# Two heads' memory queries join the key chunk, and the turns of the probabilities open the next memory step

## The chip, the cores and the metric

The kernel runs on one core of a Trainium2 chip. The metric is the device time of one execution in microseconds (us), lower is better. The engines named here are TensorE (PE in the profile, PEld for its weight loads), VectorE (DVE), ScalarE (ACT), GpSimd (POOL), and SyncE (SP), which issues DMAs. "Product" means one matmul of the program.

## The reference

Two layers of a decoder trunk on 512 tokens of width 1024, in f32. One projection `h @ w_in` feeds four branches. The change touches how two of them start, sparse attention (its keys, values and index queries) and cross-attention to a memory of 256 tokens:

```python
h = rmsnorm(x, norm_mix)
(a_x, a_b, a_c, d_q, d_k, d_v, i_q, i_k, i_w,
 g_q, g_f, g_i, g_g, m_q, gate_logits) = split_cols(h @ w_in)
y_a = a_b * causal_conv3(a_c * a_x, conv_w)
...
mq = rmsnorm(m_q.reshape(b, s, MEM_HEADS, MEM_HEAD_DIM), mem_q_norm)
ml = jnp.einsum('bshd,bmhd->bhsm', mq, mk).astype(jnp.float32) * (MEM_HEAD_DIM ** -0.5)
mp = jax.nn.softmax(ml, axis=-1).astype(mv.dtype)
y_m = jnp.einsum('bhsm,bmhd->bshd', mp, mv)
```

There are four memory heads of 128. The branches are lifted to the model's width, gated and summed, then follow an output projection, the residual and a gated FFN.

## The kernel before

Activations `h` lie feature-major: 8 blocks of 128 features by 512 tokens. Each f32 value is held as a high and a low half, and each product of two such values is three matmuls (`mm3`, L316, L317, L319: high by high, high by low, low by high). Weights come in chunks (`wchunk`): SP loads a part of 128 x 1024 raw values (four buffers), ScalarE rounds it to the high half, VectorE subtracts to get the low half (three buffers each).

A chunk is used in one of two ways. *Feature-major* (`features`): 128 columns of the weight are stationary and the 512 tokens of `h` move; the result has features on partitions. *Token-major* (`tokens`, `tokens_wide`): 128 tokens of `h` are stationary and up to 512 weight columns move; the result has tokens on partitions. `tokens` does one block of tokens after the other, `tokens_wide` takes all four blocks part by part of the weights, with an accumulator bank each. In the profile a row `mm<-h,w` is feature-major and `mm<-w,h` token-major. Eight PSUM banks serve as accumulators: three `mm`, three `tr`, two `at`.

The stretch in question is the beginning of the mixer of each layer. Three generators, written as a sequence of steps, are advanced by a string, `EARLY` (L46), letter by letter in `script`: `b` the projections of sparse attention, `c` the convolution branch, `m` the memory branch, `n` the row of norms by token (`late_norm`), `s` the selection. The string sets the order of emission; a scheduler then orders each engine's instructions by their priority and by when it takes them to be ready.

- `b`, first step: the key chunk, 256 columns (keys, values, first index queries) as four blocks by `tokens`. `key_out` evicts each block into a tile `wide` by ScalarE, scaled by the token norm `r_t`; `key_heads` normalises, rotates and transposes it (two transposes a block at L929). Later steps are the index chunk (456 columns) and the query chunk (512), both by `tokens_wide`.
- `c`, six steps of 256 columns by `features`; the evictions multiply by the norm row `r_b` (L709).
- `m`, ten steps: for each pair of heads one step with the queries (256 columns by `features`, their high and low halves, squares, four matmuls a head at L762 for the mean squares, the norm `rs`), then four steps, each half the tokens of one head: scores, maximum, exponentials, their sum and scaling (L796), four transposes of the probabilities (L798, the *turns*), products with the memory values, eviction.

In layer 1 the token norm comes first: `norm_token` (matmuls at L378) gives `r_t`, which is stored to DRAM by the ScalarE queue (L367) and loaded back as a row on all partitions by SP (L369).

`tc.add_manual_dep(..., order, ...)` sets an order of two instructions of an engine or a queue.

## Time and profile before

| | us |
|---|---|
| three runs | 1957.14, 1957.16, 1957.38 |
| median | 1957.16 |
| profiled execution | 1957.13 |
| its span, first to last instruction | 1955.4 |

The page of the profile gives busy times of the engines, the span in slices, the queues, the chain of work that ended last, and the costliest groups. Times within the trace count from the start of the span. The duration of a matmul's row is longer than its share of PE, since matmuls are pipelined: 394 ns in the largest group, while its rows start about 0.23 us apart. The DMA engines moved 386.79 MB, 198 GB/s over the span.

### The profile page before, as it was taken

The page shows a single profiled execution, that of the slowest core. Times are in us where ns is not written, and L with a number is a line of the kernel's source. Part 1 is how long each engine was busy: PE and PEld are TensorE (multiplying, and loading weights), DVE is VectorE, ACT ScalarE, POOL GpSimd, SP SyncE. Part 2 cuts the span into 40 slices and gives each one's busy share as a digit, 9 for nine tenths or more (in the row PEclk, how much of TensorE's full clock was granted, in tenths as well). Part 3 has the DMA queues.
Part 4 walks back from the last instruction along what each step waited for, and adds up shares of the span by engine and source line. Part 5 has one row for each costly group of instructions (what it writes and reads, how often), then busy time and mean ns, then how long its engine had stood idle before and what let it go on. Part 6 is the DMA issues. An engine that isn't in the chain of part 4 may idle for free.

```text
span 1955.4 us, 26140 instructions
## 1 busy us (share of the span) xinstructions
PE 1949.9 (100%) x9443; PEld 1618.5 (83%) x9443; DVE 1453.9 (74%) x2552; ACT 1166.1 (60%) x1944; POOL 232.0 (12%) x281
## 2 busy tenths in 40 slices
PE   9999999999999999999999999999999999999999
PEld 7888888878888888888888888888888888888887
DVE  7765899667776776786876688985778667867677
ACT  8654564866764556655644547477667556556464
POOL 1011111111111111110001111111111110111000
PEclk9999999999999999999999999999999999999999
DMA  9576767767777889886687776766667779898864
GB/s 365 189 185 165 178 152 171 159 143 156 178 204 193 240 229 247 248 255 191 200 215 164 180 170 157 170 163 151 153 171 177 207 199 260 240 271 249 238 187 140
DMA packets 221043, 386.79 MB, mean 198 GB/s; under 512 B 13809, under 2 KB 114417, under 8 KB 220657
## 3 DMA queue, kind: packets, MB, share of 16 engines
q1 hardware_dynamic: 162000, 247.69, 40.1%
q0 software_dynamic: 51568, 130.96, 33.2%
q10 hardware_dynamic: 7344, 6.47, 1.0%
q8 instruction: 74, 1.21, 0.3%
q14 instruction: 57, 0.46, 0.1%
HBM read 372.48 MB, written 138.42 MB: 261 GB/s over the span
## 4 chain that ended last, share of the span: by engine, by line
PE 98%; DVE 1%; DMA 0%; ACT 0%; SPq 0%; issue 0%
PE mm L316 24%; PE mm L319 24%; PE mm L317 24%; PE at L316 4%; PE at L317 4%; PE at L319 4%; PE tr L316 2%; PE tr L319 2%; PE tr L317 2%; PE tr L872 1%; PE at L832 1%; PE at L831 1%; PE tr L1592 1%; PE tr L861 1%; PE tr L929 0%; DMA w_raw<-in_mem_w_kv_dram 0%
## 5 line engine op out<-in xcount | busy, mean ns | idle before, releaser
L101 ACT ACTIVATE w_hi<-w_raw 128x1024 fp32r<-128x1024 f32 (+1 forms) x435 | 457.6, 1054 | 367.8 <-PE mm L317 129.1
L316 PE MATMUL mm<-h_hi,w_hi 128*128 128x512 f32 x960 | 378.1, 394 | 0.0
L317 PE MATMUL mm<-h_lo,w_hi 128*128 128x512 f32 x960 | 376.6, 392 | 0.0
L319 PE MATMUL mm<-h_hi,w_lo 128*128 128x512 f32 x960 | 372.8, 394 | 0.0
L1286 DVE TENSOR_TENSOR w_lo<-w_raw,w_hi 128x1024 fp32r<-128x1024 f32 x211 | 256.5, 1219 | 129.9 <-ACT w_hi L101 129.2
L245 DVE TENSOR_TENSOR w_lo<-w_raw,w_hi 128x1024 fp32r<-128x1024 f32 (+1 forms) x224 | 272.7, 1218 | 95.7 <-ACT w_hi L101 95.1
L1301 POOL DMA_DIRECT2D up_sums<-in_ffn_w_up_dram x120 | 121.4, 1012 | 832.0 <-DMA up_sums<-in_ffn_w_up_dram 561.9
L316 PEld LDWEIGHTS mm<-h_hi,w_hi 128*128 128x128 f32 x960 | 180.5, 188 | 36.5 <-DVE zq L1074 0.8
L319 PEld LDWEIGHTS mm<-h_hi,w_lo 128*128 128x128 f32 x960 | 180.2, 188 | 36.1 <-DVE w_lo L245 0.5
L317 PEld LDWEIGHTS mm<-h_lo,w_hi 128*128 128x128 f32 x960 | 180.5, 188 | 35.3
L319 PE MATMUL mm<-w_hi,h_lo 128*128 128x512 f32 (+2 forms) x408 | 151.7, 373 | 0.0
L317 PE MATMUL mm<-w_lo,h_hi 128*128 128x512 f32 (+2 forms) x408 | 151.7, 372 | 0.0
L316 PE MATMUL mm<-w_hi,h_hi 128*128 128x512 f32 (+2 forms) x408 | 145.6, 372 | 0.0
L1301 POOL DMA_DIRECT2D w_sums<-in_ffn_w_down_dram x66 | 62.3, 944 | 327.1 <-DMA w_sums<-in_ffn_w_down_dram 193.8
L316 PEld LDWEIGHTS mm<-w_hi,h_hi 128*128 128x128 f32 x408 | 76.8, 188 | 12.2 <-ACT w_hi L101 0.2
L317 PEld LDWEIGHTS mm<-w_lo,h_hi 128*128 128x128 f32 x408 | 76.9, 188 | 12.1
L319 PEld LDWEIGHTS mm<-w_hi,h_lo 128*128 128x128 f32 x408 | 76.9, 188 | 11.7
L319 PE MATMUL mm<-y_hi,w_lo 128*128 128x512 f32 x192 | 75.7, 394 | 0.0
L317 PE MATMUL mm<-y_lo,w_hi 128*128 128x512 f32 x192 | 75.3, 392 | 0.0
L316 PE MATMUL mm<-y_hi,w_hi 128*128 128x512 f32 x192 | 75.1, 393 | 0.0
L101 ACT ACTIVATE prob<-prob,small 128x128 f32<-128x128 f32 (+3 forms) x128 | 68.9, 553 | 10.3 <-DVE small L847 6.2
L317 PE MATMUL mm<-w_lo,a_hi 128*128 128x512 f32 (+1 forms) x163 | 64.0, 393 | 0.0
(462 smaller groups left out, 4193.2 us busy)
## 6 DMA issues: line engine op xcount, KB each, us to landing
w_raw<-in_w_in_dram SPq DMA_DIRECT2D x140, 512.0 KB, 4.7
up_sums<-in_ffn_w_up_dram POOLq DMA_DIRECT2D x120, 512.0 KB, 6.9
w_raw<-up_sums SPq DMA_DIRECT2D x80, 512.0 KB, 5.3
w_raw<-in_ffn_w_up_dram SPq DMA_DIRECT2D x60, 512.0 KB, 5.0
w_sums<-in_ffn_w_down_dram POOLq DMA_DIRECT2D x54, 512.0 KB, 6.6
up_sums<-up_sums POOLq DMA_DIRECT2D x40, 512.0 KB, 5.2
w_raw<-in_w_lift_dram SPq DMA_DIRECT2D x32, 512.0 KB, 4.7
w_raw<-in_ffn_w_down_dram SPq DMA_DIRECT2D x24, 512.0 KB, 5.1
```

What stands on the lines that cost most here:

```text
L101: i = act.activation(dst, src, func, **kw)
L245: i2 = dve.tensor_sub(lo, raw, f(hi))
L316: made += [pe.matmul(ps, ah, bh, start=first, stop=False, skip_group_check=more), pe.matmul(ps, ah, bl, start=False, stop=False, skip_grou ...
L317: pe.matmul(ps, ah, bl, start=False, stop=False, skip_group_check=more)]
L319: made += [pe.matmul(ps, al, bh, start=False, stop=last, skip_group_check=more)]
L831: return [pe.matmul(ps, q[:, hh, s], k[0][:, :n], start=True, stop=False), pe.matmul(ps, q[:, hh, s], k[1][:, :n], start=False, stop=True)]
L832: pe.matmul(ps, q[:, hh, s], k[1][:, :n], start=False, stop=True)]
L861: turn = pe.transpose(pp[:, (2 * e + i) * P:(2 * e + i + 1) * P], probs[2 * i + e][:, b * P:(b + 1) * P], ident)
L872: i = pe.matmul(pv[e * HD:(e + 1) * HD, c], vt[:, b, :], pt[:, b, e * 2 * P:(e + 1) * 2 * P], start=b == 0, stop=b == t)
L1286: two = A(hi, raw, AF.Copy), dve.tensor_sub(lo, raw, f(hi))
L1301: i = nc.gpsimd.dma_start(dst, src, **kw)
L1592: turns.extend(pe.transpose(ps[:, t * P:(t + 1) * P], us[t][:, j * P:(j + 1) * P], ident) for t in range(NT))
```

## The change

One weight chunk of 512 columns takes the 256 columns of keys and the 256 columns of the first two memory heads' queries, from two places of `w_in`, and is used token-major by `tokens_wide`, with the three `mm` banks and one `at` bank. `key_out` evicts the queries unscaled as well, squares them, and VectorE sums the squares to `mean_sq`. The first memory step transposes the queries, two heads by four blocks, back to feature-major, and has no chunk, no squares and no matmuls for the mean squares of its own. The second pair of heads is left as it was. In layer 1 the matmuls of the token norm are ordered behind the second of the chunk's four parts.

A memory step now yields behind the scaling; the turns, the products with the values and the evictions open the next step. The turns of a step are ordered behind the 24th matmul of the convolution chunk before it. `b` comes first in `EARLY` and has one step more. In layer 0 the move of the norm row (`row_moves[2]`) is ordered behind the second exponential instead of the fourth. The spacer of the constants shrinks by the 64 bytes that `mean_sq` takes.

```diff
-EARLY = ["mnmbmcmcbmmmsccbmscmbscmbsbbss", "mnmbmcmcbmmmsccbmscmbscmbsbbss"]
+EARLY = ["bnmbcmcmcmbmmmscbmscmbscmbsbbss", "bnmbcmcmcmbmmmscbmscmbscmbsbbss"]
...
-    consts.tile([P, 320], U8, name="spacer")
+    consts.tile([P, 256], U8, name="spacer")
...
-                if len(src.shape) == 2:
+                if isinstance(src, tuple):
+                    for g in range(2):
+                        nc.sync.dma_start(raw.rearrange("p k (g c) -> p k g c", g=2)[:, :, g, :],
+                                          src[g][k * P:e * P].rearrange("(k p) n -> p k n", p=P))
+                elif len(src.shape) == 2:
...
-    def tokens_wide(ws, a, kt, pss, first=0, in_turn=False):
+    def tokens_wide(ws, a, kt, pss, first=0, in_turn=False, marks=None):
...
                 behind_part = made[-1]
+                if marks is not None:
+                    marks.append(behind_part)
...
         def script(steps, gens):
+            filler = None
             for c in steps:
+                recent.clear()
+                turns.clear()
                 next(gens[c], None)
+                if c == "m" and filler is not None:
+                    for i in turns:
+                        tc.add_manual_dep(i.ins, filler.ins.name, order, reason="products first")
+                elif c == "c" and len(recent) >= 40:
+                    filler = recent[23]
...
-                w = wchunk(w_in[l][:, C_MQ + q * 256:C_MQ + (q + 1) * 256], KD, 256)
+                if q:
+                    w = wchunk(w_in[l][:, C_MQ + q * 256:C_MQ + (q + 1) * 256], KD, 256)
...
-                pqs = features(w, h, (0, 1))
+                if q:
+                    pqs = features(w, h, (0, 1))
+                else:
+                    pqs = [tr_ps() for _ in range(2)]
+                    for j, pq in enumerate(pqs):
+                        for t, u in enumerate(first_queries):
+                            pe.transpose(pq[:, t * P:(t + 1) * P], u[:, (2 + j) * P:(3 + j) * P], ident)
...
-                    sq = scratch512(S)
                     with tc.high_priority(offset=AHEAD):
-                        i = A(qh, pq, AF.Copy, scale=col(74 + l))
-                        if l == 0 and q == 0 and j == 0:
-                            after_two.append(i)
-                        A(sq, pq, AF.Square)
+                        A(qh, pq, AF.Copy, scale=col(74 + l))
+                        if q:
+                            sq = scratch512(S)
+                            A(sq, pq, AF.Square)
                         dve.scalar_tensor_tensor(ql, pq, col(74 + l), f(qh), op0=OP.mult, op1=OP.subtract)
-                    pm = tr_ps()
-                    for t in range(NT):
-                        pe.matmul(pm[:, t:t + 1], sq[:, t * P:(t + 1) * P], ones_h[:, 0:1], start=True, stop=True)
+                    if q:
+                        pm = tr_ps()
+                        for t in range(NT):
+                            pe.matmul(pm[:, t:t + 1], sq[:, t * P:(t + 1) * P], ones_h[:, 0:1], start=True, stop=True)
                     ms, rs = small(NT), small(NT, "mrs", 3)
-                    dve.tensor_mul(ms, pm[:, :NT], r2)
+                    dve.tensor_mul(ms, pm[:, :NT] if q else mean_sq[:, j, :], r2)
...
-                            if len(exps) == 4:
+                            if len(exps) == 2:
                                 tc.add_manual_dep(row_moves[2].ins, e.ins.name, order, reason="probabilities first")
...
                         dve.reciprocal(sm, sm)
+                        for i, p in enumerate(prs):
+                            scaled.append(dve.tensor_scalar(p, p, sm[:, i:i + 1], None, op0=OP.mult))
+                        yield
                         pp = tr_ps()
                         for i, p in enumerate(prs):
-                            scaled.append(dve.tensor_scalar(p, p, sm[:, i:i + 1], None, op0=OP.mult))
                             for b in range(2):
-                                pe.transpose(pp[:, (2 * b + i) * P:(2 * b + i + 1) * P], p[:, b * P:(b + 1) * P], ident)
+                                turns.append(pe.transpose(pp[:, (2 * b + i) * P:(2 * b + i + 1) * P], p[:, b * P:(b + 1) * P], ident))
...
-                        yield
...
                 def key_out(ps, t):
-                    u = wide()[:, :4 * HD]
+                    u = wide()
                     with tc.high_priority(offset=AHEAD):
                         A(vt[:, t, :], ps[:, HD:2 * HD], AF.Copy, scale=r_t[:, t:t + 1])
                         A(u[:, HD:2 * HD], ps[:, 0:HD], AF.Copy, scale=r_t[:, t:t + 1])
-                        A(u[:, 2 * HD:], ps[:, 2 * HD:4 * HD], AF.Copy, scale=r_t[:, t:t + 1])
+                        A(u[:, 2 * HD:4 * HD], ps[:, 2 * HD:4 * HD], AF.Copy, scale=r_t[:, t:t + 1])
+                        A(u[:, 4 * HD:], ps[:, 4 * HD:], AF.Copy)
+                    sq = scratch512(S)[:, :2 * P]
+                    A(sq, u[:, 4 * HD:], AF.Square, scale=P ** -0.5)
+                    dve.tensor_reduce(mean_sq[:, :, t], sq.rearrange("p (a b) -> p a b", b=P), axis=AX.X, op=OP.add)
                     return u
...
                 def projections():
-                    w = wchunk(w_in[l][:, C_DK:C_DK + 256], KD, 256)
-                    for t in range(NT):
-                        ps = mm_ps()[:, :256]
-                        tokens(w, h, t, ps)
-                        key_heads(key_out(ps, t), t)
+                    w = wchunk((w_in[l][:, C_DK:C_DK + 256], w_in[l][:, C_MQ:C_MQ + 256]), KD, 512)
+                    pss = [mm_ps() for _ in range(MM_BUFS)] + [at_ps()]
+                    marks = []
+                    tokens_wide([w], h, KD, pss, in_turn=True, marks=marks)
+                    for i in token_norm if l else ():
+                        tc.add_manual_dep(i.ins, marks[1].ins.name, order, reason="products first")
+                    first_queries.extend(key_out(ps, t) for t, ps in enumerate(pss))
+                    yield
+                    for t, u in enumerate(first_queries):
+                        key_heads(u, t)
                     yield
```

`mm3` collects its matmuls in `recent`, and `norm_token` its own in `token_norm`.

More of the change, by code (lines that the diff above doesn't have):

```diff
@@ L307, in tokens_wide @@
                 behind_part = made[-1]
+                if marks is not None:
+                    marks.append(behind_part)
             k0 += w.kt
+    recent, turns = [], []
     def mm3(ps, a, b, first, last, more=False, part=None):
@@ L319, in mm3 @@
             made += [pe.matmul(ps, al, bh, start=False, stop=last, skip_group_check=more)]
+        recent.extend(made)
         return made
@@ L373, in hybrid_trunk @@
     after_split = []
+    token_norm = []
     def norm_token(ssq):
         ps = tr_ps()
+        token_norm.clear()
         for t in range(NT):
-            pe.matmul(ps[:, t:t + 1], ssq[:, t * P:(t + 1) * P], ones_d, start=True, stop=True)
+            token_norm.append(pe.matmul(ps[:, t:t + 1], ssq[:, t * P:(t + 1) * P], ones_d, start=True, stop=True))
         r = small(NT, name="rstd_t", bufs=2)
@@ L698, in weave @@
                 pass
-        scaled = []
+        scaled, first_queries, mean_sq = [], [], None
         def conv_branch(y):
@@ L950, in key_out @@
                         A(u[:, HD:2 * HD], ps[:, 0:HD], AF.Copy, scale=r_t[:, t:t + 1])
-                        A(u[:, 2 * HD:], ps[:, 2 * HD:4 * HD], AF.Copy, scale=r_t[:, t:t + 1])
+                        A(u[:, 2 * HD:4 * HD], ps[:, 2 * HD:4 * HD], AF.Copy, scale=r_t[:, t:t + 1])
[3 more added lines that the diff above has]
+                    dve.tensor_reduce(mean_sq[:, :, t], sq.rearrange("p (a b) -> p a b", b=P), axis=AX.X, op=OP.add)
                     return u
                 def key_heads(u, t):
+                    u = u[:, :4 * HD]
                     w = by_head(u)
@@ L1029, in projections @@
                         yield
+                mean_sq = small(2 * NT, "mean_sq", 2).rearrange("p (j t) -> p j t", t=NT)
                 y_m, y_a = new_y(), new_y()
```

## The prediction

> **What bounds the kernel now.** I read the page first: the span, the busy times, the chain that ended last.
>
> ```profile
> span 1955.4 us, 26140 instructions
> ...
> PE 1949.9 (100%) x9443; PEld 1618.5 (83%) x9443; DVE 1453.9 (74%) x2552; ACT 1166.1 (60%) x1944; POOL 232.0 (12%) x281
> ...
> PE 98%; DVE 1%; DMA 0%; ACT 0%; SPq 0%; issue 0%
> ```
>
> TensorE is busy from one end to the other and is 98% of the chain. A busy PE can still hide lost time, since a matmul's row overlaps the next one's. So the second view is the table of waits, for PE alone (who waited for whom: us in total, times, the longest), and the third the stretches that the change touches: 54 to 82 us in layer 0 and 1003 to 1032 us in layer 1, from the first memory queries to the end of the key chunk (columns: length; PE, weight loads, VectorE, ScalarE, GpSimd busy with counts; clock; DMA share; GB/s).
>
> ```profile
> PE tr L149 <- DVE one L131: 1.2, 1, 1.2
> PE mm L317 <- DVE w_lo L245: 0.4, 1, 0.4
> PE mm L524 <- ACT w_hi L101: 0.4, 1, 0.4
> ```
>
> ```profile
> 54.00:82.00 28.00, 27.98 (x191) 25.63 (x190) 19.58 (x69) 18.55 (x49) 3.79 (x8) 1.00 0.69 224
> 1003.00:1032.00 29.00, 29.00 (x193) 26.58 (x192) 18.72 (x55) 17.41 (x49) 2.25 (x3) 1.00 0.90 187
> ```
>
> The table lists three waits, 2.0 us in the whole run, none at a turn of the probabilities (L798). PE is busy 27.98 of 28.00 us and 29.00 of 29.00 us at the full granted clock (1.00). So nothing can be won here by hiding a wait. What the change is worth is how much PE time its own instructions need, and whether a wait appears where none is. Starts in the timeline, not durations, give what a matmul costs a busy PE.
>
> **The change part by part.** First the rows of layer 0 (start, duration, engine, line, operation; x counts merged rows), and the group rows of PE for 70.68 to 76.80 us and for 185.8 to 189.3 us, which give counts.
>
> ```profile
> 54.26 0.48 PE L316 MATMUL mm<-h_hi,w_hi 128*128 128x512 f32 x1
> ...
> 55.04 0.39 PE L317 MATMUL mm<-h_lo,w_hi 128*128 128x512 f32 x1
> 55.45 0.50 PE L319 MATMUL mm<-h_hi,w_lo 128*128 128x512 f32 x1
> 55.78 0.39 PE L316 MATMUL mm<-h_hi,w_hi 128*128 128x512 f32 x1
> ...
> 65.56 0.28 PE L316 MATMUL mm<-w_hi,h_hi 128*128 128x256 f32 x1
> ...
> 67.35 0.95 PE L762 MATMUL tr<-ones_h,sq 128*128 128x1 f32 x8
> 68.16 0.36 PE L317 MATMUL mm<-w_lo,h_hi 128*128 128x256 f32 x1
> 68.36 0.28 PE L319 MATMUL mm<-w_hi,h_lo 128*128 128x256 f32 x1
> ...
> 70.69 0.28 PE L317 MATMUL mm<-w_lo,h_hi 128*128 128x256 f32 x1
> ...
> 76.81 0.60 PE L798 MATMUL tr<-ident,mprob 128*128 128x128 f32 x4
> 77.16 0.36 PE L317 MATMUL mm<-w_lo,h_hi 128*128 128x256 f32 x1
> 77.36 0.28 PE L319 MATMUL mm<-w_hi,h_lo 128*128 128x256 f32 x1
> ...
> 185.66 0.39 PE L316 MATMUL mm<-w_hi,h_hi 128*128 128x512 f32 x1
> ...
> 189.51 0.39 PE L319 MATMUL mm<-w_hi,h_lo 128*128 128x512 f32 x1
> ```
>
> ```profile
> L316 PE MATMUL mm<-w_hi,h_hi 128*128 128x256 f32 x17 | 4.8, 283 | 0.0
> L317 PE MATMUL mm<-w_lo,h_hi 128*128 128x256 f32 x17 | 4.8, 283 | 0.0
> L319 PE MATMUL mm<-w_hi,h_lo 128*128 128x256 f32 x17 | 4.8, 283 | 0.0
> ```
>
> ```profile
> L316 PE MATMUL mm<-w_hi,h_hi 128*128 128x512 f32 x6 | 2.3, 389 | 0.0
> L317 PE MATMUL mm<-w_lo,h_hi 128*128 128x512 f32 x6 | 2.3, 389 | 0.0
> L319 PE MATMUL mm<-w_hi,h_lo 128*128 128x512 f32 x5 | 1.9, 389 | 0.0
> ```
>
> *Products.* The 51 products of 256 columns between 70.69 and 76.81 us take 6.12 us, 0.120 each. The 17 of 512 columns with moving weights between 185.66 and 189.51 us take 3.85 us, 0.2265 each. Twice the columns cost 1.89 times as much: some 13 ns of each product do not depend on its width. Before, a layer computes the key chunk with 4 x 8 x 3 = 96 products of 256 columns (11.52 us) and the first two heads' queries with 2 x 8 x 3 = 48 of 512 (10.87 us), 22.39 us. Afterwards it is 96 of 512, 21.74 us: **-0.65 us** a layer, **-1.3 us** in all. Part of it is lost if the wide products run slower where they now stand: the 48 query products there, from 54.26 to 65.56 us, take 11.30 us, or 0.2296 each without the wait of 0.28 us told of below. 96 products at that pace are 22.04 us, and the saving is 0.35 a layer. So -0.7 bounds it above and -1.3 below; I take -1.3, the pace of the steady run of the same form.
>
> The Trainium skill, "TensorE: Matmul & The Clock Gate", section "Wait — 56ns, not 53.3ns?", states a fixed cost of about 2.5 ns a matmul at full clock instead. By that figure (an estimate from the page) the 48 products saved would be worth 0.12 us a layer and the merger 0.2 us instead of 1.3; the rows above give 13 ns, and the sum goes by the rows.
>
> *Norm sums.* The mean square of each of the two heads costs 4 matmuls at L762, whose eight rows run from 67.35 to 68.16 us, and the product behind them takes 0.20 us to the next start (68.16 to 68.36) instead of 0.12. That is 0.81 + 0.08 = 0.89 us a head. Four heads over two layers go: **-3.56 us**. Their place is taken by ScalarE and VectorE (below).
>
> *New transposes.* Two heads times four token blocks, 8 transposes a layer. The four at L798 take 76.81 to 77.16 us, and the product behind them 0.20 instead of 0.12: 0.35 + 0.08 = 0.43 us for four. Sixteen: **+1.72 us**.
>
> *The wait at the start of layer 0.* The third product part waits for the low half of the first weights: from 55.04 to 55.45 us and 0.33 to the next start, 0.28 us above the pace. Token-major, the part has four accumulators, whose products with the high half alone number more, so it may shrink; it may also stay. Bounds 0 and -0.28; I take **-0.1**.
>
> *The moved turns.* The scaling ends a memory step; the four transposes of a half open the next, and the order puts them behind the 24th product of the convolution chunk. That is an order on PE, not a semaphore. It gains nothing, as no turn waits now. The row of the exponentials and that of the maximum give what stands behind it:
>
> ```profile
> L101 ACT ACTIVATE mprob<-at,small,mrs 128x256 f32<-128x256 f32 x2 | 1.1, 560 | 0.2 <-DVE small L783 0.2
> L781 DVE TENSOR_REDUCE small<-at 128x2 f32<-128x512 f32 x1 | 0.7, 685 | 0.0
> ```
>
> Two exponentials and a maximum, 1.8 us, lie behind 24 products, 5.4 us. Without that cover each of the 16 halves could show its 1.8 us; the old order hides them already, so the bounds are 0 and, if the cover failed in every half, +29. **0**, by the waits table.
>
> *ScalarE, VectorE, queues.* Rows of ScalarE groups between 54 and 82 us, and one of its timeline:
>
> ```profile
> L101 ACT ACTIVATE wide<-mm,rstd_t 128x128 f32<-128x128 f32 x4 | 1.5, 371 | 0.0
> L101 ACT ACTIVATE wide<-mm,rstd_t 128x64 f32<-128x64 f32 x4 | 1.2, 309 | 0.0
> L101 ACT ACTIVATE vt<-mm,rstd_t 128x64 f32<-128x64 f32 x4 | 1.2, 308 | 0.6 <-PE mm L319 0.6
> L101 ACT ACTIVATE sq<-mm 128x512 f32<-128x512 f32 x2 | 1.2, 590 | 0.0
> ...
> 82.45 0.38 ACT L101 ACTIVATE y_hi<-at 128x256 fp32r<-128x256 f32 x1
> ```
>
> A layer gains four copies and four squares of 256 columns (0.38 each by the nearest row, 3.0 us), and loses two squares of 512 (1.2): +1.8 us on ScalarE, which has over 9 free in that stretch. VectorE gains four sums of 256 columns, under the 0.69 of the maximum over 512. Both are hidden behind 21.7 us of products; uncovered, they would cost their 2 to 3 us. A token block is now evicted by four copies, 0.31 + 0.31 + 0.37 + 0.38 = 1.4 us. In the last part each block has 6 products, so the first two blocks are complete 4.1 and 2.7 us before the chunk ends, and their banks are free for the next convolution chunk in time. The weights come as four pieces with two DMAs each instead of 2 + 2 pieces with one: four more issues a layer on SP, idle there anyway.
>
> *Added waits.* In layer 1 the token norm is put behind the second part of the chunk.
>
> ```profile
> 1003.82 0.39 PE L316 MATMUL mm<-h_hi,w_hi 128*128 128x512 f32 x1
> ...
> 1014.39 0.94 PE L378 MATMUL tr<-ones_d,ssq 128*128 128x1 f32 x8
> ...
> 1019.11 0.39 ACTq L367 DMA_DIRECT2D r_rows<-rstd_t  x1
> ...
> 1031.36 0.34 SPq L369 DMA_DIRECT2D rstd<-r_rows  x1
> ...
> DMA to landing us min/median/max: 4.6/4.6/4.6
> ```
>
> Now it starts 10.6 us into the first products; 48 wide ones end at 10.9 us. So the row is stored at about 1019, its load is issued at 1031.4 behind that store, and it lands at 1036.0, all as before. But the first convolution chunk, which needs this row to be evicted, now follows the key chunk at once: 1003.8 + 21.7 + 0.9 (token norm) = 1026.4. Its first accumulator is complete three quarters through, with the new transposes at about 1035.5, and its bank is needed only by the second accumulator of the next chunk, at about 1026.4 + 0.9 + 10.9 + 2.7 = 1040.9. The row is 4 us early. Zero, but this is the place with the least margin.
>
> **Sum**: -1.3 - 3.56 + 1.72 - 0.1 = -3.2 us. Against it I set +0.2 for small refills where new groups of transposes cut the product stream in pieces: **-3.0 us**. The profiled execution took 1957.13 us (span 1955.4 and 1.7 around it), the median of three runs is 1957.16; the forecast is **1954.1 us**.
>
> **The rivals.**
>
> *A, forecast: arithmetic alone*, PE stays full. For it: the waits table. 1953.0 to 1955.3; 58%.
>
> *B: part is given back.* The merger saves little and some turns or evictions come late: 0.6 for the slower pace of the wide products, and four or five waits of 0.3 to 0.4 us like the one at 55.04. For it: ScalarE and VectorE hold 18.55 and 19.58 of 28 us and all four token blocks now ask for them at once. Against: the 4.1 and 2.7 us of lead. It gives 1955.3 to 1957.6, about 1956.3; 17%. By the page's 2.5 ns the same sum would land at 1955.2.
>
> *C, slower: the norm row.* In layer 1 SP issues in order and stands from 1019 to 1031.4 for the store. If the store goes out later, or the load is queued behind weight loads that wait for a buffer, the row comes after 1041 and PE stops one us for each us, with the weight loads behind it late too. From -3.0 it needs 7 us, a row at 1048, to be slower by over 0.2%; then about 1962. Against: store and load stand in the order they had, with 4 us of margin. 8%.
>
> *D: more than the arithmetic.* Layer 0's wait goes whole (0.2 more), the 0.2 set against the sum is not paid, and the two 0.4 us waits of the table, or as much at places that it does not list, go as the schedule shifts: another 1.2 us, 1952.9 and below; 17%.
>
> That the change does not do what it says would show as unmoved turns; it would not alter the time, since the turns never waited.
>
> **How the numbers follow.** 0.2% is 3.9 us, about what a measurement can tell from no change: below 1953.2 is faster, above 1961.1 slower. D and a slice of A (0.05) lie below: 0.22. C lies above: 0.08. The rest, 0.70, is within: a real gain, too small for the bound. The range leaves out C and the outer half of D, 16% in all: 1952.3 to 1957.6.
>
> **What would show it.** Right: 96 products of 128x512 `mm<-w,h` in place of 256-wide ones, about 0.227 apart; 32 rows fewer at the norm sums; 16 transposes more of `wide`; PE still at 28 of 28 us in both stretches; no new wait above 0.5 us. Wrong: a PE wait for `rstd` or a convolution accumulator near 1041 (C); waits for ScalarE copies of `wide` at the chunk's end (B).

## The result, and the profile after

| | before | after |
|---|---|---|
| median, us (range, runs) | 1957.15 (1957.13 to 1957.38, 4) | 1986.4 (1985.28 to 1986.49, 4) |
| profiled execution, us | 1957.13 | 1985.28 |
| its span, us | 1955.4 | 1983.6 |
| mean granted clock | 1.00 | 0.993 |

The ratio is 1.0148, with a 95% interval of 1.013 to 1.0165. The change costs 29.25 us where 3.0 were forecast to be won, and the time lies far outside the range. The page of the changed kernel (span; busy times; the engines' shares of the chain that ended last):

```profile
span 1983.6 us, 25934 instructions
...
PE 1958.2 (99%) x9331; PEld 1614.7 (81%) x9331; DVE 1457.0 (73%) x2560; ACT 1169.3 (59%) x1956; POOL 231.8 (12%) x281
...
PE 96%; DVE 3%; ACT 1%; issue 0%; DMA 0%; SPq 0%; ACTq 0%
```

TensorE has 112 rows fewer, which is what the change promises: 48 products less in each layer, 32 rows of norm sums less, 16 transposes more. VectorE has 3% of the chain in place of 1%. The table of PE's waits (who waited for whom: us in total, times, longest), which had three entries of 2.0 us in all, now begins:

```profile
PE tr L957 <- DVE wide L942: 8.1, 4, 3.4
PE at L859 <- ACT wide L101: 4.6, 6, 1.1
PE mm L324 <- ACT wide L101: 2.7, 2, 1.4
PE at L324 <- ACT mpt_hi L101: 1.4, 2, 0.7
PE mm L536 <- ACT w_hi L101: 1.3, 2, 1.1
PE mm L324 <- DVE gate L729: 1.2, 1, 1.2
```

L957 is the transposing of the rotated query heads (L929 before), L859 the selection scores, L942 the end of the rotation. To see where the time went, I took for every PE row the time to the next row's start, and split it into the steady pace of its form (0.227 us for 512 columns, 0.120 for 256, 0.109 for a transpose, and so on) and the excess. Steady work fell from 1932.6 to 1929.5 us, by 3.1; it is counts times paces, so it restates the arithmetic of the prediction. What is measured is the excess, which rose from 18.0 to 49.5 us, by 31.5. (The level of both depends on the paces taken for the short forms; the differences between runs don't.)

| excess of PE, us | before | after |
|---|---|---|
| layer 0, key chunk and first halves (54 to about 165 us) | 0.6 | 3.2 |
| layer 0, rest of the four branches (to 270; 280 after) | 0.5 | 14.7 |
| layer 1, first part of the same | 0.4 | 0.5 |
| layer 1, rest of the same | 0.4 | 14.7 |
| everything else | 16.1 | 16.4 |

Of the two 14.7, 13.0 each lie in the last 40 us of the stage. The prediction had looked at 54 to 82 us and at 1003 to 1032 us, the beginnings. The same end of the stage, by stretches (length; PE, weight loads, VectorE, ScalarE, GpSimd busy; granted clock; DMA share; GB/s), first before:

```profile
236.00:262.00 26.00, 26.00 (x129) 21.96 (x129) 25.19 (x52) 19.34 (x38) 4.36 (x6) 1.00 0.59 132
1186.00:1212.00 26.00, 26.00 (x129) 21.98 (x128) 25.11 (x51) 19.35 (x40) 3.77 (x4) 1.00 0.63 150
```

and after:

```profile
252.00:255.00 3.00, 2.60 (x14) 1.88 (x12) 3.00 (x11) 1.20 (x5) 0.02 (x1) 1.00 0.67 87
255.00:257.00 2.00, 1.12 (x4) 0.59 (x4) 1.75 (x4) 1.98 (x6) 0.56 (x1) 1.00 0.05 8
257.00:258.50 1.50, 0.51 (x2) 0.44 (x2) 1.47 (x5) 0.61 (x2) 0.00 (x0) 0.82 0.53 164
258.50:260.00 1.50, 0.83 (x4) 0.35 (x4) 1.50 (x6) 0.49 (x1) 0.80 (x1) 0.50 0.00 0
260.00:264.00 4.00, 0.82 (x4) 0.42 (x2) 3.94 (x11) 1.68 (x3) 0.56 (x1) 0.50 0.45 66
264.00:267.00 3.00, 2.11 (x9) 1.71 (x9) 2.87 (x8) 1.19 (x2) 0.52 (x1) 0.50 0.30 87
267.00:270.00 3.00, 2.81 (x9) 2.08 (x10) 2.89 (x8) 1.23 (x3) 0.28 (x1) 0.50 0.62 86
```

Two things are to be seen. VectorE was 97% busy at the stage's end before the change already (25.19 of 26.00 us): it rotates query heads there, sums selection scores and makes low halves of weights. That cost nothing, because PE had products to run meanwhile. Afterwards VectorE is as busy, but PE has run out: 0.82 us of work between 260 and 264. And from about 258 us the clock is granted at 0.50, so what PE does until 270 goes at half pace. The timeline of PE shows what it works on (in brackets the idle time before a row, and its releaser):

```profile
252.46 0.39 PE L327 MATMUL mm<-h_hi,w_lo 128*128 128x512 f32 x1
...
254.23 0.60 PE L957 MATMUL tr<-ident,wide 128*128 128x128 f32 x4
255.88 0.44 PE L859 MATMUL at<-ik_hi,iqS 128*128 128x384 f32 x1 [1.05 <-ACT wide L101]
...
259.74 1.09 PE L957 MATMUL tr<-ident,wide 128*128 128x128 f32 x4 [0.67 <-DVE wide L942]
264.20 1.12 PE L957 MATMUL tr<-ident,wide 128*128 128x128 f32 x4 [3.38 <-DVE wide L942]
265.11 1.06 PE L827 MATMUL tr<-ident,mprob 128*128 128x128 f32 x4
266.86 0.58 PE L324 MATMUL at<-mpt_hi,mv 128*128 128x256 f32 x1 [0.69 <-ACT mpt_hi L101]
...
270.58 1.05 PE L324 MATMUL mm<-y_hi,w_hi 128*128 128x512 f32 x2
```

From 252.7 to 270.6 us no chunk of weights is multiplied at all; only selection scores, transposes and the last half of the memory branch are left. That half's turns start at 265.1. The turns of the probabilities in layer 0, all eight halves, as one row of the tile's view (ns min/median/max; first and last start), before and after:

```profile
L798 PE MATMUL tr<-ident,mprob x32: 270/272/273, 76.8 to 238.4; 128*128 128x128 f32 x32
```

```profile
L827 PE MATMUL tr<-ident,mprob x32: 270/272/421, 106.7 to 265.8; 128*128 128x128 f32 x32
```

The first scores of the branch come at 88.7 in place of 67.1 us, the first turns 30 us later, the last turns 27 us later.

### The profile page after: what moved, and what is told of

The parts are those of the page before. It is cut to its first block, busy times and chain, and to the rows that moved or that the text cites. A ratio compares the mean times of both kernels' runs of the same rounds, so it can differ in the third digit from the quotient of the medians.

```text
span 1983.6 us, 25934 instructions
## 1 busy us (share of the span) xinstructions
PE 1958.2 (99%) x9331; PEld 1614.7 (81%) x9331; DVE 1457.0 (73%) x2560; ACT 1169.3 (59%) x1956; POOL 231.8 (12%) x281
## 4 chain that ended last, share of the span: by engine, by line
PE 96%; DVE 3%; ACT 1%; issue 0%; DMA 0%; SPq 0%; ACTq 0%
PE mm L324 23%; PE mm L325 23%; PE mm L327 23%; PE at L325 4%; PE at L327 4%; PE at L324 4%; PE tr L324 2%; PE tr L327 2%; PE tr L325 2%; PE tr L900 1%; PE tr L1631 1%; PE tr L889 1%; PE at L859 1%; PE at L860 1%; DMA w_raw<-in_mem_w_kv_dram 0%
## 5 line engine op out<-in xcount | busy, mean ns | idle before, releaser
L101 ACT ACTIVATE w_hi<-w_raw 128x1024 fp32r<-128x1024 f32 (+2 forms) x435 | 457.4, 1054 | 383.6 <-PE mm L325 120.9
L324 PE MATMUL mm<-h_hi,w_hi 128*128 128x512 f32 x928 | 365.0, 394 | 4.0 <-ACT wide L101 2.7
L325 PE MATMUL mm<-h_lo,w_hi 128*128 128x512 f32 x928 | 363.6, 392 | 0.0
L327 PE MATMUL mm<-h_hi,w_lo 128*128 128x512 f32 x928 | 358.6, 393 | 0.0
L324 PEld LDWEIGHTS mm<-h_hi,w_hi 128*128 128x128 f32 x928 | 174.4, 188 | 40.6 <-ACT wide L101 3.2
L327 PEld LDWEIGHTS mm<-h_hi,w_lo 128*128 128x128 f32 x928 | 174.3, 188 | 35.6 <-issue 0.6
L325 PEld LDWEIGHTS mm<-h_lo,w_hi 128*128 128x128 f32 x928 | 174.4, 188 | 34.6 <-issue 0.4
L325 PE MATMUL mm<-w_lo,h_hi 128*128 128x512 f32 (+1 forms) x392 | 152.6, 389 | 0.3 <-DVE w_lo L249 0.3
L327 PE MATMUL mm<-w_hi,h_lo 128*128 128x512 f32 (+1 forms) x392 | 152.5, 389 | 0.0
L324 PE MATMUL mm<-w_hi,h_hi 128*128 128x512 f32 (+1 forms) x392 | 146.2, 388 | 0.0
L101 ACT ACTIVATE prob<-prob,small 128x128 f32<-128x128 f32 (+3 forms) x128 | 69.9, 556 | 23.7 <-DVE small L875 18.6
L662 DVE TENSOR_TENSOR gate<-mm,rstd 128x512 f32<-128x512 f32 x64 | 43.8, 688 | 28.3 <-PE mm L327 28.1
```

Of the source, the lines that this page charges most:

```text
L101: i = act.activation(dst, src, func, **kw)
L324: made += [pe.matmul(ps, ah, bh, start=first, stop=False, skip_group_check=more), pe.matmul(ps, ah, bl, start=False, stop=False, skip_grou ...
L325: pe.matmul(ps, ah, bl, start=False, stop=False, skip_group_check=more)]
L327: made += [pe.matmul(ps, al, bh, start=False, stop=last, skip_group_check=more)]
L662: dve.tensor_mul(g, ps, r_b)
```

## The experiments

**Theory 1**: the string has ten `m`. When a step ended with its eviction, the tenth finished the branch (letter 24 of 30). Now a step ends with the scaling, the tenth `m` only gives the last half's scores, and its turns, products and eviction come when `script` empties the generators behind the whole string, after three more `b` and three more `s`. The lift of the memory branch waits for them. **Theory 2**: three `c` instead of two stand ahead of the index chunk; the selection scores start 12.7 us later (176.2 for 163.5 us) and crowd VectorE and ScalarE at the end.

All fifteen runs, each against runs of the kernel before on the same chip (medians 1957.1 to 1957.9). "First" is the first memory score of layer 0, "turns" the last start of its turns, "excess" is counted as above, over the whole run.

| run | what | us | ratio (95% interval) | first | turns | excess |
|---|---|---|---|---|---|---|
| before | | 1957.15 | | 67.1 | 238.4 | 18.0 |
| after | | 1986.4 | 1.0148 (1.013, 1.0165) | 88.7 | 265.8 | 49.5 |
| 1 | eleventh `m` | 1972.95 | 1.0077 (1.0047, 1.0106) | 88.5 | 254.0 | 35.6 |
| 2 | index chunk earlier | 1982.37 | 1.0125 (1.0095, 1.0154) | 88.0 | 263.6 | 46.5 |
| 3 | turns not moved | 1969.85 | 1.0058 (1.0036, 1.0081) | 88.3 | 246.1 | 32.0 |
| 4 | before, turns moved | 1982.98 | 1.0128 (1.0098, 1.0157) | 67.1 | 264.0 | 43.7 |
| 5 | chunk, old places | 1977.07 | 1.0096 (1.0079, 1.0113) | 87.4 | 250.9 | 42.5 |
| 6 | 4 with eleventh `m` | 1969.04 | 1.0059 (1.0039, 1.0079) | 67.2 | 254.1 | 29.6 |
| 7 | 1 and 2 | 1965.82 | 1.0047 (1.0031, 1.0063) | 92.2 | 255.3 | 33.2 |
| 8 | 1, norm row earlier | 1973.32 | 1.0081 (1.0061, 1.0101) | 88.7 | 254.6 | 35.9 |
| 9 | 7, two swaps | 1967.15 | 1.0046 (1.0026, 1.0066) | 89.6 | 253.0 | 31.2 |
| 10 | 9, norm row earlier | 1965.02 | 1.004 (1.0021, 1.006) | 88.3 | 250.2 | 28.5 |
| 11 | 7 without the edge | 1965.67 | 1.0036 (1.0016, 1.0056) | 90.3 | 253.3 | 31.3 |
| 12 | 9, index chunk still earlier | 1985.39 | 1.0142 (1.0113, 1.0172) | 88.7 | 262.9 | 48.9 |
| 13 | 10, last half sooner | 1964.7 | 1.0038 (1.0022, 1.0054) | 88.6 | 250.5 | 28.8 |
| 14 | 13, selection behind `c` | 1964.1 | 1.0032 (1.0016, 1.0048) | 88.2 | 250.3 | 28.6 |
| 15 | before, new string in layer 1 | 1974.56 | 1.0088 (1.0059, 1.0118) | 69.9 | 241.2 | 36.4 |

None is faster than the kernel before. (Run 15's layer 0 has the string of the kernel before; its branch starts 2.8 us later by waits ahead of 54 us. The profiled execution of run 7 is the slowest of its three, 1969.01 us, and its excess is that of this execution.)

Two sets of these runs are the same program in effect. The rows of TensorE, ScalarE and VectorE come in the same order, row for row (buffer numbers left out), in runs 10, 13 and 14, and so they do in runs 7 and 11: the scheduler undid what these edits changed. Differences within a set (0.9 and 0.2 us of median) are noise.

### Runs 1 to 4: the last half or the index chunk

Run 1, an eleventh `m` ahead of the last query heads (the last letters `b` handle one block of query heads each):

```diff
-"bnmbcmcmcmbmmmscbmscmbscmbsbbss"
+"bnmbcmcmcmbmmmscbmscmbscmbsmbbss"
```

> The changed kernel with one more memory step in the order string, ahead of the last four letters, so that the last half of the fourth memory head (turns, products with the values, eviction) is emitted before the last query heads instead of after everything. Theory 1 (the last half is emitted too late, and the lift of the memory branch, which needs it, leaves TensorE without products near 255 and 1217 us): those waits, 14 us a layer, go, and the time falls by 22 to 28 us to 1958 to 1964, with the small waits near 96 and 191 us left. Theory 2 (the index chunk stands behind a third convolution step, so the selection starts 12 us later and crowds VectorE at the end of the stage): the time stays above 1978.

Run 2, the index chunk (the third `b`) ahead of the third `c`:

```diff
-"bnmbcmcmcmbmmmscbmscmbscmbsbbss"
+"bnmbcmcmbcmmmmscbmscmbscmbsbbss"
```

> The changed kernel with the index chunk moved ahead of the third convolution step, as many convolution steps before it as in the old order; still ten memory steps, so the last half is still emitted last. Theory 1: the waits at the end of the stage stay, time above 1978. Theory 2: the scores start about 11 us earlier, VectorE is less crowded at the end, and the time falls by 20 us or more, below 1966.

Run 3, the changed kernel with the `yield` back behind the eviction (the order that puts turns behind the 24th product, called the edge below, stays):

```diff
                             scaled.append(dve.tensor_scalar(p, p, sm[:, i:i + 1], None, op0=OP.mult))
-                        yield
                         pp = tr_ps()
...
                         dve.tensor_sub(y_m[1][:, hh, d], py, f(y_m[0][:, hh, d]))
+                        yield
```

> The changed kernel, but a memory step ends with the eviction of its half, as before the change; chunk and order string as in the changed kernel, so ten steps finish all memory work. Theory 1: the waits at the end of the stage go and the time is 1957 to 1965 (matmul work 3 us below the old kernel, new waits in other places from turns that stand right behind their scaling). Theory 2: the order of convolution and index chunk is unchanged, so the time stays above 1976.

Run 4, the kernel before with this `yield` moved ahead of the turns and nothing else (no edge):

> The old kernel with the moved yield alone: the turns open the next memory step; chunk, queries and the old order string with ten memory steps as before. Theory 1: the last half of the fourth head is emitted last here too, so the time rises by 15 to 28 us, to 1972 to 1985, with waits at the end of the stage in both layers. Theory 2: the selection starts as before, and the time stays within 4 us of 1957.

Run 4 decides the most: without the new chunk, with the old string, the moved turns alone cost 25.6 us, where the whole change costs 29. Its waits for PE, in its own line numbers (L930 is the transposing of heads):

```profile
PE tr L930 <- DVE wide L915: 10.2, 3, 4.9
PE tr L800 <- DVE mprob L795: 2.3, 1, 2.3
```

It is the changed kernel's picture: PE stands at the rotated heads, and the last turns are at 264.0 us. Of its 25.7 us of excess over the kernel before, 21.6 lie at the ends of the two stages. The other 4.1 lie at 93 to 106 us of layer 0, where the turns of one half wait 2.3 us and the clock is then at 0.50 for 3.4 us. In layer 0, run 1 moves nothing of the branch but its last turns, from 265.8 to 254.0 us, and returns 13.5 us; the wait at the heads goes from 8.1 to 2.7 us:

```profile
PE tr L957 <- DVE wide L942: 2.7, 2, 1.4
```

So theory 1 names the bulk, and run 2 refutes theory 2 as the main cause: an earlier index chunk alone returns 4.0 us. But runs 1 and 3 came out between the two forecasts, 9 and 5 us above the upper end that theory 1 allowed them. Theory 1 was not the whole. With the turns back in their step, run 3 still lies 12.7 us above the kernel before, and its longest waits are turns behind their scaled probabilities, one half in each layer:

```profile
PE tr L826 <- DVE mprob L822: 4.6, 2, 2.3
```

So neither place of the turns suits the new order: moved, the last half comes too late; unmoved, a half of each layer has no cover.

### Runs 5 to 8: the rest

Run 5 keeps the new chunk and puts all else where it stood: `yield` at the end, no edge, the old string with `b n m` in front.

```diff
-"bnmbcmcmcmbmmmscbmscmbscmbsbbss"
+"bnmmbmcmcbmmmsccbmscmbscmbsbbss"
```

> The new chunk with the old places of everything else: a memory step yields at its end as before, no edge for the turns, and the order is the old string with the chunk and the first memory step put in front of what stood second (b n m, then m b m c m c b and so on as of old). Theory 1 (all of the loss comes from places in the order: late last half, query chunk in the middle of the selection scores, three halves without products between them; the chunk itself only saves products): the waits of the third run at 122, 196, 1076 and 1151 us go, excess falls from 32 to 18 to 21 us, time 1953 to 1958. Rival (the chunk itself costs, by its evictions and its norm row): the waits stay whatever the order, 1964 to 1972.

Run 6 is run 4 with an eleventh `m` ("...scmbsmbbss"); like run 4 it has no edge:

> The kernel before with only the moved yield, and an eleventh memory step ahead of the last two query chunks. Theory 1 (the ten letters leave the last half to the drain): the 25.6 us of the moved yield alone fall to under 10, 1957 to 1967. If the eleventh letter only repairs half, as it did for the changed kernel (13.5 us), 1968 to 1972, and what is left is the half still behind the last step of selection. Rival (the turns behind 24 products are themselves what costs): over 1975.

Run 7 joins runs 1 and 2 ("bnmbcmcmbcmmmmscbmscmbscmbsmbbss"):

> The changed kernel with both strings' edits: an eleventh memory step and the index chunk one convolution step earlier. If late half and late index chunk are separate costs, their gains add: 1986.4 - 13.5 - 4.0 = about 1969. If the index chunk matters only once the last half is in time, more: 1960 to 1966. If both relieve the same wait, 1972 to 1974.

Run 8 is run 1 with the copy of the norm row in layer 0 behind the second copy of the first queries, not behind the second exponential:

```diff
-                        A(qh, pq, AF.Copy, scale=col(74 + l))
+                        i = A(qh, pq, AF.Copy, scale=col(74 + l))
+                        if l == 0 and q == 0 and j == 1:
+                            tc.add_manual_dep(row_moves[2].ins, i.ins.name, order, reason="queries first")
...
-                            if len(exps) == 2:
-                                tc.add_manual_dep(row_moves[2].ins, e.ins.name, order, reason="probabilities first")
```

> The first run (changed kernel with the eleventh memory step, 1972.95) with the copy of the norm row on ScalarE ordered behind the second copy of the first queries in place of the second exponential. If the 2.1 us of waits at 95 to 98 us of layer 0 are the row's place (VectorE's gate product waits for the row, its bank holds the next products up), 1970.5 to 1971.5, and the wait of the products for the gate tile is gone; if the row is late by its transfer or the gate bank has another cause, 1973, the wait stays.

Run 5 missed by 19 us, lies above its rival's range too, and is the most instructive miss. Its excess at the stage's end is gone, but 100 to 140 us of layer 0 holds 13 us now, and the same place in layer 1 holds 10 (windows, then PE's waits; L952 transposes heads, L986 ends the key heads, L821 are the turns):

```profile
104.00:125.00 21.00, 12.34 (x49) 10.35 (x48) 13.22 (x45) 7.53 (x23) 2.52 (x4) 0.67 0.64 149
```

```profile
PE tr L952 <- DVE wide L986: 7.1, 2, 4.7
PE tr L821 <- DVE mprob L817: 4.5, 3, 2.2
```

Between the scores of a half and its turns stand a maximum, two exponentials, a sum's reciprocal and two scalings, on two engines in turn. PE can only pass that time with products of other branches. In the old order the query products ran first, from 54.3 to 65.3 us, and the 96 products of the key chunk behind them (11.5 us) covered norm, scores and softmax of the first half: 51 of them stand right ahead of its turns. The merged chunk runs both at once, so its products are spent when the first scores can begin, at 87.4 us. With the old order behind it, the key heads (on VectorE) and the halves meet at 104 to 125 us, and the products do not last. This is read from the trace; no run puts other products into that place.

Run 6 returns 13.9 us of 25.6, as run 1 did: half. The excess that it keeps over the kernel before, 11.6 us, is the 4.2 at 90 to 110 us and 3.6 and 3.8 at the ends of the stages. Run 7 returns more than the sum of its parts by the medians (20.6 for 13.5 + 4.0), so the index chunk's place seems to count once the last half is in time; its slowest execution returns 17.4, no more than the sum, but the four of run 11, the same order, lie at 1965.0 to 1967.1. Run 8 does nothing for the time: the wait for the gate tile is gone, but turns wait for their scaled probabilities at 118 to 120 us:

```profile
PE tr L827 <- DVE mprob L822: 2.3, 1, 2.3
```

### Runs 9 to 12: neighbours

Run 9 swaps two pairs of letters of run 7, run 10 adds run 8's edit to run 9, run 11 is run 7 without the edge, run 12 puts the index chunk of run 9 two letters sooner, ahead of the second `c`.

```diff
-"bnmbcmcmbcmmmmscbmscmbscmbsmbbss"   (run 7)
+"bnmbcmcmbcmmmmscmbscmbscmbmsbbss"   (runs 9, 10)
+"bnmbcmbcmcmmmmscmbscmbscmbmsbbss"   (run 12)
```

> The run with the eleventh step and the earlier index chunk (1965.8), with two neighbours swapped: the memory step ahead of the query chunk that followed it, and the last memory step ahead of the last step of selection. Theory 1 (what is left are places in the order): the wait of about 1.5 us per layer at 193 and 1140 us and part of the 3.6 us per layer at 240 to 262 and 1200 to 1220 us go: 1960 to 1963. If the last turns then still come 15 us later than in the kernel before, because the memory branch starts 21 us later (first scores at 88 in place of 67 us), no more than 1 us is gained: 1964 to 1967.

> The same as the ninth kernel with the norm row's copy behind the second copy of the first queries. If the 2.46 us wait that came up at 117 us in the eighth kernel belongs to that order alone, 1.2 to 2 us less than the ninth; if the half-step chain has no cover there in any order, the same time as the ninth within 1 us and a wait of turns on the scaled probabilities between 100 and 125 us.

> The run with the eleventh step and the earlier index chunk (1965.8), without the edge that holds the turns behind the 24th product of the last convolution step. If the edge gives the turns their cover, waits of turns on the scaled probabilities come up, 1967 to 1972; if it holds the branch back, 1960 to 1964; if the place of the step alone matters, within 1 us.

> As the ninth, with the index chunk ahead of the second convolution step. Theory 2 as a part (the selection scores come 12.7 us late and meet the query chunk's evictions on ScalarE): selection starts some 8 us sooner than in the ninth, 1957 to 1962. If the halves of the memory branch lose their cover by it, waits of turns on the scaled probabilities at 110 to 130 and 1065 to 1085 us, 1965 to 1972.

Run 9 gained nothing: its runs (1966.58 to 1968.25) overlap run 7's (1965.63 to 1969.01). Run 10 is 2.1 us below run 9 (their executions just touch, 1966.61 and 1966.58), about what layer 0's wait for the norm row had cost; here no wait of the turns took its place. Run 11 has the time and the order of run 7, so there the edge binds nothing; what it would be worth where it binds, no run shows. Run 12 loses 18 us to run 9 by one letter and missed both its forecasts: its turns begin at 131.2 instead of 106.0 us, but they hardly wait. PE waits for key heads at 91 to 97 us, where the index chunk now stands (3.6 and 1.3 us, and the clock is at 0.50 from 96 to 103 us), and later, in each layer, selection scores wait for the exponentials of a half, and a half's products for the copy of its probabilities:

```profile
PE tr L957 <- DVE wide L991: 3.6, 1, 3.6
PE at L859 <- ACT mprob L101: 3.5, 2, 2.0
PE at L324 <- ACT mpt_hi L101: 2.8, 4, 0.7
```

### Runs 13 to 15: what is left, and chunk against order

Run 13 puts the last half's scores ahead of the last `c`, run 14 also the first step of selection behind a `c`. Run 15 is the kernel before with the changed kernel's string in layer 1 alone.

```diff
-"bnmbcmcmbcmmmmscmbscmbscmbmsbbss"   (run 10)
+"bnmbcmcmbcmmmmscmbscmbsmcbmsbbss"   (run 13)
+"bnmbcmcmbcmmmmcsmbscmbsmcbmsbbss"   (run 14)
```

> The tenth kernel (1965.0) with the last half's scores put ahead of the last convolution step, its turns still behind a query chunk. If the last half's place is what is left at 240 to 262 and 1200 to 1220 us (3.5 us of excess in each layer), 1958 to 1961; if the lift of the memory branch waits for something else there (the weights of the query chunks, the bank of the scores), 1964 to 1966.

> As the thirteenth, with the first step of selection behind a convolution step in place of ahead of it. If the 1.8 us per layer at 168 and 1122 us (selection scores wait for the bank that VectorE reads for the memory output) go with that place, 3 to 4 us less than the thirteenth: 1954 to 1958, the time of the kernel before or less; otherwise the same as the thirteenth, or up to 5 us more where selection ends late.

> The kernel before (key chunk and memory queries as two chunks, memory step yielding at its end) with the changed kernel's order string in layer 1 alone. The third run, which has that order and the merged chunk, loses 6.7 us in layer 1. If it is the order that loses them (memory chain 21 us later), about 1957.3 + 6.7 = 1962 to 1966, with the first memory scores of layer 1 some 20 us later than before; if it is the merged chunk (its 48 products no longer stand between the halves), 1956 to 1959.

Runs 13 and 14 stay within 1 us of run 10: the scheduler makes the same order of these strings, so neither settles its question. What run 14 still waits for, beyond the old waits:

```profile
PE at L859 <- DVE y_lo L838: 3.0, 4, 0.9
PE at L324 <- ACT mpt_hi L101: 1.4, 2, 0.7
```

These lie at 169, 250 to 259 us and the same places of layer 1, and hold 1.9 and 3.5 us of excess in each layer, 10.9 together. That accounts for the 7 us that it lacks to the kernel before and the 3.1 us of work that it saves.

Run 15 was to tell order and chunk apart, and it does not. It costs 17.4 us, 8.6 above the upper end of its forecast, and by the excess some 15 of them lie in layer 1 (nearly 4 at its start, 4 at 1099 and 8 at 1210 us). But the string means something else there. In the kernel before, the key heads belong to the first step of `b`; in the changed kernel they are a second step. So from the second `b` on, each letter brings the next step of sparse attention too early. The first product of the index chunk in layer 1 stands at 1056.2 us in the kernel before; in run 15 and in run 3, which has this string and the merged chunk, at

```profile
1034.46 0.36 PE L316 MATMUL mm<-w_hi,h_hi 128*128 128x456 f32 x1
```

```profile
1069.74 0.36 PE L324 MATMUL mm<-w_hi,h_hi 128*128 128x456 f32 x1
```

An index chunk that comes sooner cost 18 us in run 12 too. So run 15 says nothing of the merged chunk; whether the changed kernel's order would be slow with two chunks stays open. That the merged chunk cannot do with the old order is run 5.

## Why the prediction was wrong

*The moved turns* are the step that failed: "It gains nothing, as no turn waits now", "**0**, by the waits table", with +29 if the cover failed in every half. Alone they cost 25.6 us (run 4). Neither of the two reasons considered is the main cause: run 4 has no edge behind the 24th product at all, and it is not sixteen halves that lose 1.8 us each. One half of run 4 does lose its cover, with a wait of 2.3 us (the 1.8 left out the reciprocal and the two scalings). A step that yields earlier finishes its work one letter later, and with ten letters the last half has no letter left. In the changed kernel 13 us of excess stand at the end of each layer's stage, and no turn waits for its probabilities. The prediction counted letters nowhere, and looked for a stall only at the turn, not at who needs its result last, the lift of the memory branch. The waits table could not show this: it shows what waits now, not by how much the others miss waiting. The window of 236 to 262 us, VectorE busy 25.19 of 26.00, would have shown that PE lived there on other branches' products.

*The new order* had no cost in the sum either: "the old order hides them already" was said of an order that the change replaces. With the turns unmoved it still loses 12.7 us (run 3), and the merged chunk in the old order loses 19.6 (run 5); in both, turns wait for their probabilities, 4.6 and 4.5 us. How much of this is the chunk's and how much the order's is not shown.

*The place looked at.* Both stretches were at the stage's beginning. There the forecast nearly held: up to the first halves, 0.5 us of excess in layer 1 and 3.2 in layer 0, most of it the norm row at 95 us told of below.

*Products.* Right, in kind and in size. The new chunk in layer 0 (PE's timeline):

```profile
54.42 0.70 PE L324 MATMUL mm<-w_hi,h_hi 128*128 128x512 f32 x2
54.96 0.40 PE L324 MATMUL at<-w_hi,h_hi 128*128 128x512 f32 x1
55.62 0.51 PE L325 MATMUL mm<-w_lo,h_hi 128*128 128x512 f32 x1 [0.26 <-DVE w_lo L249]
55.96 0.40 PE L327 MATMUL mm<-w_hi,h_lo 128*128 128x512 f32 x1
...
76.61 0.39 PE L327 MATMUL at<-w_hi,h_lo 128*128 128x512 f32 x1
76.84 0.38 PE L776 MATMUL tr<-ident,wide 128*128 128x128 f32 x2
```

From 54.42 to 76.84 are 22.42 us. The stretch from 54.96 to 55.96 holds 0.54 above the pace of two rows; the prediction reckoned its 0.28 in the same way. The 96 products thus take 21.88, 0.228 each, between the pace taken and the slower one. Before, the 48 query products took 11.02 there and the key chunk 11.52, so the saving is 0.66 in this layer, as forecast. The prediction's other bound, 0.35, took the slower pace after the change but the faster one before it; with the slower pace for both it is 0.50.

*The wait at the start of layer 0* grew from 0.28 to 0.54 us instead of falling by 0.1.

*Norm sums and new transposes* came out as counted: 32 rows gone, 16 added. *ScalarE and VectorE* hide the evictions of the chunk, and the transposes follow at 76.84 without a gap: of rival B's waits at the chunk's end there is none. The 0.2 us set against the sum for refills had no row behind it, and no run singles it out.

*Rival C*, the norm row in layer 1, did not come: the row's load is issued at 1047.5, lands 5.4 us later, and PE waits for nothing there. VectorE waits 1.7 us for it and has the time. It is layer 0 in which the row costs, about 2 us (runs 9 and 10; run 8 gains nothing by it): the changed order puts its copy behind the second exponential, and that comes at 95 us, where the fourth one, which it followed before, came at 89. The prediction listed this edit among the changes and gave it no cost.

*The sum.* Excess 31.5 less 3.1 of work is 28.4, the growth of the span by 28.2. As far as runs tell, 13.5 come back with the last half (run 1), 7.1 more with the index chunk's place (run 7), and 1 to 2 more with two swaps and the norm row (runs 10, 13 and 14, one order). The last 7 us over the kernel before lie at two named places in each layer; which order would free them was not found.

## What to carry to other kernels

In an order written by hand, moving a step's boundary changes where *every* later part of it is emitted: count the letters that each generator gets, and look at who receives the last one. A string carried over to a kernel whose steps are cut otherwise means something else (run 15), and different strings can give the same order (runs 10, 13 and 14): compare the emitted rows before reading a time. Before costing a reordering at zero because "nothing waits", look at the end of the stage for the engine that is nearly full beside the full one: its work is hidden by products that the reordering may spend earlier. And work that is removed or moved ahead may have been the cover of something (read from run 5's trace); ask for each product taken out of the middle what ran beside it.

## What was not expected of the hardware

The granted clock fell to 0.50 at 258.0 us of the changed kernel without a long pause. In the 3.4 us ahead of it PE was busy 1.42 us, with waits of 1.05 and 0.99 us; the wait of 3.38 us came afterwards. In run 4 it fell at 102.1 us, 0.8 us after a wait of 2.30 us had ended, with PE busy 1.10 of the 3.4 us before; run 3 stayed at 1.00 through a wait of 2.30 us that ended at 125.0. In run 5 it stayed at 1.00 over a wait of 1.09 us and fell at 110.9, 2.6 us into one of 4.72 us. The Trainium skill, "TensorE: Matmul & The Clock Gate", section "What's actually happening", has the clock at half rate after an idle window of about 3.4 us. The 0.50 agrees with its half rate; in the changed kernel and in run 4 the fall came without an idle time of that length.

In the changed kernel the clock stood at 0.50 for 13.6 us in layer 0 and 13.8 in layer 1; runs 1, 7 and 10, whose mean clock is 1.00, are spared this. PE's rows in each of these stretches are 4.0 us of work at the steady pace, so that, as an estimate, up to 4 of the 13 us at each stage's end are the clock and not the wait.
